# Layer 1's r, v and z projections on one Trainium2 core: TensorE in emission order, with the systems' work at set places between portions of twelve products

## The chip, the cores and the metric

The kernel runs on 1 core of one Trainium2 chip. The metric is the device time of one execution in microseconds. The engines are TensorE (PE, matrix products), VectorE (DVE), ScalarE (ACT), GpSimd (POOL) and SyncE (SP), which issues the DMAs of this kernel. Each engine works its instructions off in its own order, and waits where an operand or a buffer is not ready.

## The reference

One inference step of a trunk with two layers, 1,104 rows (16 meta tokens, 1,024 prompt rows and 8 x 8 sample rows) of width 1,024. Layer 0 is a gated DeltaNet, layer 1 an RWKV-7 time mixing. Of layer 1, with the shapes D = 1024 and 16 heads of 64:

```python
def rwkv_mixer(xn, S0, shift_prev, mu, w_rkvz, w0, w1, w2, a0, a1, a2, k_k, k_a, r_k, lnx_w, lnx_b, w_o):
    xprev = jnp.concatenate([shift_prev[:, None].astype(jnp.float32), xn[:, :-1]], 1)
    xx = xprev - xn
    xs = xn[None] + xx[None] * mu[:, None, None, :]
    rkvz = jnp.einsum('sbtd,sde->sbte', xs[:4], w_rkvz)
    r, k, v, z = rkvz[0], rkvz[1], rkvz[2], rkvz[3]
    w = -jax.nn.softplus(-(w0 + jnp.tanh(xs[4] @ w1) @ w2)) - 0.5
    a = jax.nn.sigmoid(a0 + (xs[5] @ a1) @ a2)
    kk = l2norm((k * k_k).reshape(B, T, H, N))
    ...
    def step(S, inp):
        S = (S * d_t[:, :, None, :]
             + jnp.einsum('bhvk,bhk->bhv', S, -kk_t)[..., None] * b_t[:, :, None, :]
             + v_t[..., None] * k_t[:, :, None, :])
        return S, jnp.einsum('bhvk,bhk->bhv', S, r_t)
```

The kernel doesn't step through the rows. It cuts them into chunks of 64, and for each chunk and head solves a triangular system of 64 x 64 whose matrix comes from the keys kk, the rates a and the decays. Inverting these matrices needs k, a and w alone, not r, v or z, so it can be done while r, v and z are projected.

## The kernel before

The rows stand in three segments of 384, 384 and 336 columns (`SEGS`). Layer 1 first projects k, the decays and the rates (`keys_decay_rate`), then r, v and z, and then runs the wave over the chunks. The part from k's end to the wave's start is the stage of the change.

*Projections.* For each of m = 0 (r), 2 (v) and 3 (z), `mix` builds the shifted input of that m in pairs of tiles (xa, xc, xh are high parts, xl and others low parts), 8 parts a segment: ACT scales (mixs), DVE adds (L1071, L1068), ACT casts to the high part (L86) and DVE or POOL subtracts for the low part (L90). Then `project(m, k, ...)` makes the 8 output tiles. The weights of a tile come in two halves (wraw; `load_w`, L202), split by ACT into whi and by POOL into wlo, three buffers each. A segment's product is 24 matmuls into one tile d in PSUM (`dense`): 8 slices of the inner dimension, each with whi by high, wlo by high and whi by low. ACT copies d to ev (L1155), and SP stores it (L1156). r and v have three segments, z two; z's third is left to the wave, for which `gate_inputs` prepares the input.

*Systems.* There are 24 items (3 segments by 8 pairs of heads), worked on in five batches of 5, 5, 5, 5 and 4 by `rwkv_inverse`, called after the projection tiles 1, 4, 7, 10 and 13 of the 24. An item loads its cs, a and k (sldcs, slda, sldk, L1255), and prepares its keys: sal (DVE, L1273), skk (POOL, then DVE, L1299). PE then makes the scores: 12 small matmuls fL and one product frss with a head mask. The scores are copied (sgl, ACT; rkc, DVE, L1313) and stored to DRAM by SP (rltd, L1311; rssd, L1314). When a batch's items are stored, `block_scale` loads the norms back (invR, L487; bblk, L492), PE transposes invR into fbpp (called bpp here), and DVE forms rk and bblk (L494, L495). `inverse_blocks` loads the blocks of the systems (L21, L456; invA, L461), scales them (L462), inverts 32 x 32 blocks in 31 pairs of DVE steps (`inverse32`, L444 and L446: a batch's inverse), copies (ACT, L464), stores both (r_t, L468, and r_u, L467), and loads them in the form that the merge needs: T1n (L472) and per item sTT (four loads, L478, after a POOL memset, L476). `inverse_merge` joins the blocks of an item: 12 matmuls mY, a DVE scaling into invY (L510, twice), 12 matmuls mU, ACT into sTT, then SP's store ttd (L1322). The wave reads ttd.

*Buffers.* sTT has three buffers for the five items of a batch, so items 3 and 4 wait until the stores ttd of items 0 and 1 have landed. T1n, L21, invT, sal have one buffer, skk and sgl two. PSUM has four buffers for d, two for the f tiles (L, rss, bpp, lora) and two for mY and mU.

*Order.* In this stage a scheduler decides the order of every engine's instructions, PE's too: products of several tiles and the systems' work stand interleaved in it as it estimated them to be ready. The wave behind already stands in a manual order for PE (`tc.manual_schedule`), in which PE's instructions stand as they are emitted.

Of the kernel before, what the change touches and what calls it, by code (L numbers as in the profile page):

```python
# [16 lines left out]
SEGS = [(0, 384), (384, 384), (768, 336)]  # L17
# [18 lines left out]
class Builder:  # L36
# [461 lines left out]
    def inverse_merge(self, L21, TT, T1n, scale_col, pool, th0, n):  # L498

        nc = self.nc  # L500
        pY = self.ps("m", 2, "Y")
        yv = pY[:, 0:32 * n].rearrange("p (c i) -> p c i", i=32)
        for c in range(n):
            for p in (0, 1):
                a = 64 * p
                self.mm(yv[a + 32:a + 64, c, :], L21[a:a + 32, th0 + c, :], T1n[a:a + 32, th0 + c, :])
        Y = self.t(pool, [128, 192], "invY", 2)[:, 0:32 * n].rearrange("p (c i) -> p c i", i=32)
        for p in (0, 1):
            a = 64 * p + 32
            nc.vector.tensor_tensor(Y[a:a + 32], yv[a:a + 32],  # L510
                                    scale_col[a:a + 32].unsqueeze(2).broadcast_to([32, n, 32]), op=ALU.mult)
        pU = self.ps("m", 2, "U")
        uv = pU[:, 0:32 * n].rearrange("p (c i) -> p c i", i=32)
        for c in range(n):
            for p in (0, 1):
                a = 64 * p
                self.mm(uv[a:a + 32, c, :], Y[a + 32:a + 64, c, :], TT[a + 32:a + 64, c, 32:64])
        for p in (0, 1):
            a = 64 * p
            self.act(TT[a:a + 32, :, 32:64], uv[a:a + 32], AF.Identity, scale=-1.0)  # L520
# [621 lines left out]
            self.mm(p[:, 0:n], wl, h[:, c0:c0 + n], start=False, stop=True)  # L1142
            dst(k, s, p)

    def project(self, m, k, x, dst, apart=False):

        nc, t = self.nc, self.t
        w = self.load_w(self.i["rwkv_w_rkvz"][0, m][:, 128 * k:128 * k + 128])
        ps = (self.dense(w, 128, *x, s, bufs=4) for s in range(2 if m == 3 else 3)) if apart else self.dense3(w, 128, *x)
        for (c0, n), p in zip(SEGS, ps):  # L1150
            f = t(self.ev, [128, 384], "ev", 3)
            if m == 3:
                self.gate(f[:, 0:n], p[:, 0:n])
            else:
                nc.scalar.copy(f[:, 0:n], p[:, 0:n])  # L1155
            nc.sync.dma_start(dst[k][:, c0:c0 + n], f[:, 0:n])  # L1156

    def keys_decay_rate(self, x, hh, hl):

        nc, t, i, col = self.nc, self.t, self.i, self.pcol  # L1160
        with self.tc.tile_pool(name="lora", bufs=1, reuse_waits="tile") as pool:
            z = t(pool, [128, 8, 48], "zpad")
            nc.gpsimd.memset(z, 0.0)
            for d in (self.ad, self.rd, self.vd, self.zd, self.kd):
                nc.sync.dma_start(d[:, :, NT:1152].rearrange("k p n -> p k n"), z)
            sm = t(pool, [128, 384], "sm0")
            sm1 = t(pool, [128, 384], "sm1")
            self.scan_mask(sm, True)
            self.scan_mask(sm1, False)

            wr = t(pool, [128, 2, D], "lw2")
            for q in (0, 64):
                nc.sync.dma_start(wr[q:q + 64, 0], i["rwkv_w2"][0])
                nc.sync.dma_start(wr[q:q + 64, 1], i["rwkv_a2"][0])
            w2 = t(pool, [128, 2, D], "lw2h", dt=F32R), t(pool, [128, 2, D], "lw2l", dt=F32R)
            nc.scalar.copy(w2[0], wr)

            for u, q in ((0, slice(0, 64)), (1, slice(64, 128))):
                nc.vector.tensor_tensor(w2[1][q, u], wr[q, u], w2[0][q, u].bitcast(F32), op=ALU.subtract)
                nc.gpsimd.memset(w2[1][64 - q.start:128 - q.start, u].bitcast(F32), 0.0)  # L1180

            def dst_w(k, s, p):
                c0, n = SEGS[s]
                f = t(self.ev, [128, 384], "ev", 3)
                if s == 2:
                    nc.gpsimd.memset(f[:, n:384], 0.0)
                self.act(f[:, 0:n], p[:, 0:n], AF.Sigmoid, bias=col["rwkv_w0"][:, k:k + 1])
                g = t(pool, [128, 384], "ev2", 2)
                nc.vector.tensor_tensor_scan(g, sm if s == 0 else sm1, f, 0.0, op0=ALU.mult, op1=ALU.add)
                nc.sync.dma_start(self.csd[k][:, c0:c0 + 384], g)  # L1190

            def dst_a(k, s, p):
                c0, n = SEGS[s]
                f = t(self.ev, [128, 384], "ev", 3)
                self.act(f[:, 0:n], p[:, 0:n], AF.Sigmoid, bias=col["rwkv_a0"][:, k:k + 1])
                nc.sync.dma_start(self.ad[k][:, c0:c0 + n], f[:, 0:n])
            for k in range(8):
                self.project(1, k, x, self.kd, k in (0,))
                self.lora_second(0, k, hh, w2, dst_w)
                self.lora_second(1, k, hl, w2, dst_a)  # L1200

# [76 lines left out]

    ahead = None

    def rwkv_inverse(self, b, pool):

        items = range(5 * b, min(5 * b + 5, 24))
        nth = 6 * len(items)
        nc, t = self.nc, self.t
        ltd, ssd = self.dram([nth, 128, 64], f"rltd{b}"), self.dram([nth, 128], f"rssd{b}")
        for q, n in enumerate(items):
            s, p = divmod(n, 8)
            names = ("cs", "a", "k")
            ld = self.ahead or self.rwkv_load(n, pool, "s", names)  # L1290
            kk, Dp, iD = self.rwkv_keys(p, ld, pool, "s")

            self.ahead = self.rwkv_load(n + 1, pool, "s", names) if n < 23 else None
            sq = t(pool, [128, 384], "sgl", 2)
            self.act(sq, kk, AF.Square)
            al = t(pool, [128, 6, 64], "sal", 1)
            self.alpha(al, kk, Dp, s, nc.vector)
            nc.gpsimd.tensor_tensor(kk, kk, ld["a"], op=ALU.mult)
            nc.vector.tensor_tensor(kk, kk, iD, op=ALU.mult)  # L1299
            gp = self.ps("f", 2, "L")  # L1300
            ssp = self.ps("f", 2, "rss")
            for c in range(6):
                for h in (0, 1):
                    a = 64 * h
                    self.mm(gp[a:a + 64, 64 * c:64 * c + 64], kk[a:a + 64, 64 * c:64 * c + 64], al[a:a + 64, c, :])
            self.mm(ssp[0:2, 0:384], self.hmask, sq)
            gl = t(pool, [128, 6, 64], "sgl", 2)
            nc.scalar.copy(gl, gp[:, 0:384].rearrange("p (c i) -> p c i", i=64))
            if s == 0:
                nc.gpsimd.tensor_tensor(gl[:, 0, :], gl[:, 0, :], self.m_strs2, op=ALU.mult)  # L1310
            nc.sync.dma_start(ltd[6 * q:6 * q + 6].rearrange("c q i -> q c i"), gl)  # L1311
            kc = t(pool, [2, 384], "rkc", 1)
            nc.vector.tensor_copy(kc, ssp[0:2, 0:384])  # L1313
            nc.sync.dma_start(ssd[6 * q:6 * q + 6].rearrange("c (h i) -> h c i", h=2), kc.rearrange("h (c i) -> h c i", c=6))  # L1314
        rk2 = self.rk2[:, 30 * b:30 * b + nth]
        blk = self.block_scale(ssd, rk2, pool)
        TT = [t(pool, [128, 6, 64], "sTT", 3) for _ in items]
        T1n, L21 = t(pool, [128, 30, 32], "T1n", 1), t(pool, [128, 30, 32], "L21", 1)
        self.inverse_blocks(f"r{b}", ltd, blk, pool, TT, T1n[:, 0:nth], L21[:, 0:nth], nth)
        for q, n in enumerate(items):  # L1320
            self.inverse_merge(L21, TT[q], T1n, rk2[:, 6 * q:6 * q + 6], pool, 6 * q, 6)
            nc.sync.dma_start(self.ttd[n], TT[q].rearrange("p c k -> p (c k)"))  # L1322


    def rwkv_front(self, p, s):
# [415 lines left out]
    def layer1(self, ctx, right, stay, xa, xb, x):  # L1741

        nc, tc = self.nc, self.tc
# [2 lines left out]
        self.keys_decay_rate(x, self.hh, self.hl)  # L1746
        ip = pool("rinv", ctx)
        self.rwkv_masks(ip, True)
        todo = [(m, k) for m in (0, 2, 3) for k in range(8)]
        slots = {0: (0, 1, 2, 3, 4, 5, 9, 10), 2: (6, 7, 8, 0, 1, 2, 9, 10), 3: range(3, 11)}  # L1750
        for n, (m, k) in enumerate(todo):
            if k == 0:
                x = self.mix(m, xb, slots[m], SEGS[0:2] if m == 3 else SEGS)
            self.project(m, k, x, {0: self.rd, 2: self.vd, 3: self.zd}[m], k in range(8))
            if n in (1, 4, 7, 10, 13):
                self.rwkv_inverse((1, 4, 7, 10, 13).index(n), ip)
            if n == 16:
                zin = self.gate_inputs(xa, xb)
        ctx.close()
        right.close()  # L1760
        self.psum_pool()
# [14 lines left out]
        last.close()  # L1776
        ctx.close()
        self.psum.close()

    def wave(self, zin, stay, last, pool):  # L1780

# [109 lines left out]
```

## Time and profile before

| | us |
|---|---|
| median of 3 runs | 2412.91 |
| lowest and highest run | 2412.68, 2417.64 |
| the profiled execution's own time | 2422.7 |
| its span in the profile | 2421.0 |
| mean granted PE clock of that execution | 0.967 |

Beside the lines that the prediction shows, these are the page's chain of waits (the work that ended last, by engine) and its view of the span in 40 slices, of which the stage is about slices 25 to 31:

```profile
PE 17%; DVE 6%; DMA 3%; issue 2%; ACT 1%; POOL 1%; SPq 0%; DVEq 0%; POOLq 0%; ACTq 0%
...
PE   6989999999999999999989998988998888888896
DVE  6868676776868596863347616588894567667654
PEclk9999999999999999999999999999998999999998
```

How rows of the trace are read. A line of a timeline is: start in us, duration in us, engine (SPq is SP's DMA queue), source line, operation, output<-inputs, shapes and count; in brackets the idle time before it and what ended it. A row of a windows view is: the window, its length, then per engine busy us and the count of instructions, the granted PE clock (1.00 is full), the share of DMA engines in use and GB/s. Matmuls are pipelined, so their durations overlap.

### The profile page before, as it was taken

How to read it: one execution, taken by the hardware profiler on the slowest of the kernel's cores; microseconds unless marked ns; L12 is line 12 of the kernel's file. 1: busy time of each engine (PE TensorE's matmuls, PEld its weight loads, DVE VectorE, ACT ScalarE, POOL GpSimd, SP SyncE). 2: the span in 40 equal slices, each digit the busy share in tenths (PEclk: the TensorE clock that was granted, in tenths of full speed). 3: DMA queues.
4: the chain of work that ended last, by engine and by line, in shares of the span. 5: the costliest groups of instructions: out<-in, count | busy, mean ns of one | idle time of the engine just before them, and what ended most of it. 6: DMA issues, size and time to landing. Idle time of an engine off the chain costs nothing. (4 is left out here: it accounts for less than half of the span.)

```text
span 2421.0 us, 54809 instructions
## 1 busy us (share of the span) xinstructions
PE 2213.4 (91%) x19737; PEld 2003.7 (83%) x19737; DVE 1620.5 (67%) x4201; ACT 1279.8 (53%) x3665; POOL 1049.8 (43%) x1446
## 2 busy tenths in 40 slices
PE   6989999999999999999989998988998888888896
PEld 5888989888898989888989898877787676777775
DVE  6868676776868596863347616588894567667654
ACT  5445555555646565565334647474453555666552
POOL 3435343334434353433314424453354555666643
PEclk9999999999999999999999999999998999999998
DMA  3323333323232333353351344666645435555543
GB/s 110 104 74 101 86 109 86 91 76 99 82 108 61 100 96 89 94 160 114 108 137 61 97 172 153 169 160 172 167 122 173 124 107 149 158 163 156 157 131 117
DMA packets 470924, 290.05 MB, mean 120 GB/s; under 512 B 188506, under 2 KB 456027, under 8 KB 470651
## 3 DMA queue, kind: packets, MB, share of 16 engines
q1 hardware_dynamic: 470650, 286.53, 42.0%
q8 instruction: 156, 2.56, 0.5%
q14 instruction: 118, 0.96, 0.1%
HBM read 200.53 MB, written 85.89 MB: 118 GB/s over the span
## 5 line engine op out<-in xcount | busy, mean ns | idle before, releaser
L90 POOL TENSOR_TENSOR wlo<-wraw,whi 128x512 fp32r<-128x512 f32 (+2 forms) x252 | 331.8, 1319 | 379.9 <-ACT whi L86 361.6
L76 PE MATMUL d<-xc,whi 128*128 128x384 f32 (+2 forms) x910 | 258.3, 341 | 4.5 <-POOL xc L90 2.5
L86 ACT CAST whi<-wraw 128x512 fp32r<-128x512 f32 (+2 forms) x252 | 152.0, 605 | 145.4 <-PE dq L76 50.7
L411 DVE SCALAR_TENSOR_TENSOR cvy<-raw,cw,cvy 128x408 f32<-128x408 f32 (+2 forms) x288 | 179.0, 634 | 16.3 <-ACT cvy L62 14.5
L76 PEld LDWEIGHTS d<-xc,whi 128*128 128x128 f32 (+1 forms) x910 | 167.5, 191 | 10.7 <-issue 3.4
L444 DVE TENSOR_TENSOR invtmp<-invA,invT 72x31 f32<-72x31 f32 (+31 forms) x403 | 165.2, 410 | 14.1 <-DMA invA<-ltd 5.3
L446 DVE TENSOR_TENSOR invT<-invT,invtmp 72x31 f32<-72x31 f32 (+31 forms) x403 | 165.7, 411 | 6.6
L76 PE MATMUL dz<-xc,whi 128*128 128x384 f32 (+1 forms) x480 | 148.9, 341 | 0.0
L76 PE MATMUL dv<-xc,whi 128*128 128x384 f32 (+1 forms) x480 | 146.8, 335 | 0.0
L76 PE MATMUL d<-xc,wlo 128*128 128x384 f32 (+2 forms) x428 | 142.3, 341 | 1.4 <-POOL wlo L90 1.4
L76 PE MATMUL d<-xa,whi 128*128 128x384 f32 (+3 forms) x450 | 139.8, 345 | 3.5 <-DVE xa L90 1.7
L860 POOL TENSOR_SCALAR Sb<-Sb,eglb 128x128 f32<-128x128 f32 x128 | 80.1, 643 | 90.4 <-DMA Sb<-in_state_gdn 46.8
L76 PE MATMUL dv<-xa,whi 128*128 128x384 f32 (+1 forms) x288 | 100.0, 347 | 0.1
L76 PE MATMUL dz<-xa,whi 128*128 128x384 f32 (+1 forms) x288 | 100.1, 348 | 0.0
L76 PEld LDWEIGHTS d<-xa,whi 128*128 128x128 f32 (+1 forms) x450 | 83.1, 190 | 11.5 <-issue 4.5
L76 PEld LDWEIGHTS dz<-xc,whi 128*128 128x128 f32 x480 | 89.4, 192 | 0.8
L76 PEld LDWEIGHTS dv<-xc,whi 128*128 128x128 f32 x480 | 88.6, 188 | 0.5 <-issue 0.4
L80 PE MATMUL rA<-UV,G 128*64 128x64 f32 x1152 | 63.6, 240 | 26.0 <-DVE rS L1470 24.0
L76 PE MATMUL d<-xa,wlo 128*128 128x384 f32 (+3 forms) x252 | 85.5, 339 | 0.0
L62 ACT ACTIVATE o<-rA,gcol 128x128 f32<-128x128 f32 x128 | 46.6, 372 | 73.6 <-DVE S L771 73.3
L76 PE MATMUL d<-xh,wlo 128*128 128x384 f32 (+1 forms) x256 | 84.1, 344 | 1.5 <-POOL wlo L90 1.5
L76 PE MATMUL d<-xh,whi 128*128 128x384 f32 (+1 forms) x256 | 84.2, 344 | 0.7 <-ACT whi L86 0.4
(509 smaller groups left out, 7194.7 us busy)
## 6 DMA issues: line engine op xcount, KB each, us to landing
wraw<-in_gdn_w_in SPq DMA_DIRECT2D x96, 256.0 KB
wraw<-in_rwkv_w_rkvz SPq DMA_DIRECT2D x80, 256.0 KB
Sb<-in_state_gdn SPq DMA_DIRECT2D x64, 256.0 KB
wraw<-in_rwkv_w_o SPq DMA_DIRECT2D x40, 256.0 KB
E<-drow SPq DMA_DIRECT2D x24, 384.0 KB
attn<-drow SPq DMA_DIRECT2D x24, 384.0 KB
wraw<-in_gdn_w_out SPq DMA_DIRECT2D x36, 256.0 KB
out_s_gdn<-Sb SPq DMA_DIRECT2D x32, 256.0 KB
```

The lines of the kernel that those rows point to most:

```text
L62: return self.nc.scalar.activation(out, in_, func, bias=bias, scale=scale, **kw)
L76: self.nc.tensor.matmul(out, lhsT, rhs, start=start, stop=stop)
L80: self.nc.tensor.matmul(out, lhsT, rhs, start=start, stop=True, skip_group_check=True)
L86: nc.scalar.copy(hi, x)
L90: e.tensor_tensor(lo, x, hi.bitcast(F32), op=ALU.subtract)
L411: nc.vector.scalar_tensor_tensor(y[:, 0:wd], raw[:, k:k + wd], cw[k], y[:, 0:wd], op0=ALU.mult, op1=ALU.add)
L444: nc.vector.tensor_tensor(tmp, A[:, j, j + 1:32].unsqueeze(2).broadcast_to([nb, n, m]), Tv[:, j, 0:m].unsqueeze(1).broadcast_to([nb, n, m] ...
L446: nc.vector.tensor_tensor(Tv[:, j + 1:32, 0:m], Tv[:, j + 1:32, 0:m], tmp, op=ALU.subtract)
L860: nc.gpsimd.tensor_scalar(Sb[:, u], Sb[:, u], self.eglb[:, hv, 4 * g + u:4 * g + u + 1], None, op0=ALU.mult)
```

## The change

The loop over r, v and z moves into a method `projections`, which stands under `tc.manual_schedule` for PE: PE's order in the stage is now the order of emission. A segment's 24 matmuls are emitted as two portions of twelve, one for each half of the weights, and after each portion `gap()` is called. There are six gaps in a tile of r or v and four in one of z, 128 in all.

`gap()` takes one step of the systems. `rwkv_inverse` is a generator now: for each item, the loads and the keys are emitted, three gaps are left for them, and then the scores stand. Behind a batch's last scores four gaps are left, then the transpose and the whole inverse are emitted. The merges are put off: merge n of a batch starts (mY) 28 + n gaps after the batch's inverse was emitted, and its second half (mU, the store ttd) stands one gap later, behind a `yield` in `inverse_merge`. The orders of DVE, ACT, POOL and SP stay with the scheduler, which now finds PE's order given. Batches follow one another every 19 gaps: each has five items of three gaps, and four gaps before the transpose. The projection of k's first tile keeps its form with an empty gap.

```diff
     def inverse_merge(self, L21, TT, T1n, scale_col, pool, th0, n):
...
+        yield
         pU = self.ps("m", 2, "U")
...
-    def project(self, m, k, x, dst, apart=False):
+    def project(self, m, k, x, dst, gap=None):
...
-        w = self.load_w(self.i["rwkv_w_rkvz"][0, m][:, 128 * k:128 * k + 128])
-        ps = (self.dense(w, 128, *x, s, bufs=4) for s in range(2 if m == 3 else 3)) if apart else self.dense3(w, 128, *x)
-        for (c0, n), p in zip(SEGS, ps):
+        his, los = w = self.load_w(self.i["rwkv_w_rkvz"][0, m][:, 128 * k:128 * k + 128])
+        ps = zip(SEGS, self.dense3(w, 128, *x)) if gap is None else ((c, self.ps("d", 4)) for c in SEGS[0:2 if m == 3 else 3])
+        for (c0, n), p in ps:
+            if gap is not None:
+                c = 0
+                for q in range(8):
+                    wh, wl = his[q // 4][:, q % 4], los[q // 4][:, q % 4]
+                    a, b = x[0][q][:, c0:c0 + n], x[1][q][:, c0:c0 + n]
+                    for l, r in ((wh, a), (wl, a), (wh, b)):
+                        self.mm(p[:, 0:n], l, r, start=c == 0, stop=c == 23)
+                        c += 1
+                    if q % 4 == 3:
+                        gap()
...
-    def rwkv_inverse(self, b, pool):
+    def rwkv_inverse(self, b, pool, merges):
...
+            for _ in range(3):
+                yield
             gp = self.ps("f", 2, "L")
...
+        for _ in range(4):
+            yield
         rk2 = self.rk2[:, 30 * b:30 * b + nth]
...
-        for q, n in enumerate(items):
-            self.inverse_merge(L21, TT[q], T1n, rk2[:, 6 * q:6 * q + 6], pool, 6 * q, 6)
-            nc.sync.dma_start(self.ttd[n], TT[q].rearrange("p c k -> p (c k)"))
+        def merge(q):
+            m = self.inverse_merge(L21, TT[q], T1n, rk2[:, 6 * q:6 * q + 6], pool, 6 * q, 6)
+            next(m)
+            yield
+            next(m, None)
+            nc.sync.dma_start(self.ttd[items[q]], TT[q].rearrange("p c k -> p (c k)"))
+        merges.extend(merge(q) for q in range(len(items)))
...
-        todo = [(m, k) for m in (0, 2, 3) for k in range(8)]
-        for n, (m, k) in enumerate(todo):
-            if k == 0:
-                x = self.mix(m, xb, slots[m], SEGS[0:2] if m == 3 else SEGS)
-            self.project(m, k, x, {0: self.rd, 2: self.vd, 3: self.zd}[m], k in range(8))
-            if n in (1, 4, 7, 10, 13):
-                self.rwkv_inverse((1, 4, 7, 10, 13).index(n), ip)
-            if n == 16:
-                zin = self.gate_inputs(xa, xb)
+        with tc.manual_schedule(engines={mybir.EngineType.PE}):
+            zin = self.projections(xa, xb, ip)
...
+    def projections(self, xa, xb, ip):
+        slots = {0: (0, 1, 2, 3, 4, 5, 9, 10), 2: (6, 7, 8, 0, 1, 2, 9, 10), 3: range(3, 11)}
+        now, wait, under, merges = [0], [], [], []
+        def systems():
+            for b in range(5):
+                yield from self.rwkv_inverse(b, ip, merges)
+                wait.extend((now[0] + 28 + n, m) for n, m in enumerate(merges))
+                merges.clear()
+        sy = systems()
+        def gap():
+            now[0] += 1
+            for m in under:
+                next(m, None)
+            under.clear()
+            while wait and wait[0][0] <= now[0]:
+                m = wait.pop(0)[1]
+                next(m)
+                under.append(m)
+            next(sy, None)
+        for m in (0, 2, 3):
+            x = self.mix(m, xb, slots[m], SEGS[0:2] if m == 3 else SEGS)
+            for k in range(8):
+                self.project(m, k, x, {0: self.rd, 2: self.vd, 3: self.zd}[m], gap)
+                if (m, k) == (3, 0):
+                    zin = self.gate_inputs(xa, xb)
+        while wait or under:
+            gap()
+        return zin
```

More of the change, by code (lines that the diff above doesn't have):

```diff
@@ L1197, in keys_decay_rate @@
             for k in range(8):
-                self.project(1, k, x, self.kd, k in (0,))
+                self.project(1, k, x, self.kd, (lambda: None) if k == 0 else None)
                 self.lora_second(0, k, hh, w2, dst_w)
@@ L1748, in layer1 @@
         self.rwkv_masks(ip, True)
-        todo = [(m, k) for m in (0, 2, 3) for k in range(8)]
-        slots = {0: (0, 1, 2, 3, 4, 5, 9, 10), 2: (6, 7, 8, 0, 1, 2, 9, 10), 3: range(3, 11)}
-        for n, (m, k) in enumerate(todo):
-            if k == 0:
-                x = self.mix(m, xb, slots[m], SEGS[0:2] if m == 3 else SEGS)
-            self.project(m, k, x, {0: self.rd, 2: self.vd, 3: self.zd}[m], k in range(8))
-            if n in (1, 4, 7, 10, 13):
-                self.rwkv_inverse((1, 4, 7, 10, 13).index(n), ip)
-            if n == 16:
-                zin = self.gate_inputs(xa, xb)
+        with tc.manual_schedule(engines={mybir.EngineType.PE}):
+            zin = self.projections(xa, xb, ip)
         ctx.close()
```

## The prediction

> **What bounds the kernel now.** I read the page first, then windows, waits and timelines of the one stage that the change touches.
>
> ```profile
> span 2421.0 us, 54809 instructions
> PE 2213.4 (91%) x19737; PEld 2003.7 (83%) x19737; DVE 1620.5 (67%) x4201; ACT 1279.8 (53%) x3665; POOL 1049.8 (43%) x1446
> ```
>
> TensorE (PE) is busy for 91% of the span. The stage runs from r's first product of tile 0 to z's last product. The windows view over it, over the stretch from bpp(1) to bpp(2) (the transpose into tile bpp that ends batch 1's and batch 2's collection) and over four slices gives busy time by engine, then the granted PE clock:
>
> ```profile
> core 0: us, PE busy (x) PEld busy (x) DVE busy (x) ACT busy (x) POOL busy (x), PEclk, DMA share, GB/s
> 1464.20:1857.30 393.10, 359.46 (x3331) 316.18 (x3329) 284.86 (x599) 205.83 (x444) 171.51 (x256) 0.95 0.61 159
> 1599.41:1660.31 60.90, 54.31 (x561) 46.40 (x559) 56.05 (x115) 39.46 (x91) 30.14 (x39) 0.93 0.68 167
> 1598.00:1602.00 4.00, 4.00 (x52) 3.11 (x52) 3.33 (x9) 2.68 (x6) 1.03 (x1) 0.50 0.31 50
> 1602.00:1606.00 4.00, 4.00 (x16) 3.58 (x15) 3.17 (x5) 3.75 (x9) 3.33 (x4) 0.65 0.70 144
> 1482.00:1486.00 4.00, 2.71 (x9) 2.00 (x8) 2.92 (x6) 4.00 (x10) 2.96 (x6) 0.50 0.45 129
> ```
>
> The stage is 393.1 us: PE is idle for 393.1 − 359.5 = 33.6, and a mean clock of 0.95 costs 0.05 × 393.1 = 19.7 more. PE's own work is then 393.1 − 33.6 − 19.7 = 339.8 us. VectorE (DVE) is close behind where a mix and an inverse meet: 56.05 of 60.9 us. The lines view of PE over the stage (count | busy us, mean ns of one | idle before, and what ended it), its main rows:
>
> ```profile
> L76 PE MATMUL d<-xc,whi 128*128 128x384 f32 (+1 forms) x400 | 115.5, 345 | 2.7 <-POOL xc L90 2.5 <-DVE xc L90 0.2
> L76 PE MATMUL d<-xa,whi 128*128 128x384 f32 (+1 forms) x288 | 83.9, 345 | 3.5 <-DVE xa L90 1.7 <-ACT xa L86 1.3 <-ACT whi L86 0.5
> L76 PE MATMUL d<-xc,wlo 128*128 128x384 f32 (+1 forms) x200 | 69.5, 348 | 1.4 <-POOL wlo L90 1.4
> ...
> L76 PE MATMUL fL<-sal,skk 64*64 64x64 f32 x576 | 25.1, 235 | 11.1 <-DVE skk L1299 11.0
> L76 PE MATMUL frss<-sgl,hmask 128*2 128x384 f32 x48 | 21.3, 527 | 1.9 <-DVE rk L494 1.9
> L76 PE MATMUL mU<-sTT,invY 32*32 32x32 f32 x576 | 16.6, 195 | 3.3 <-ACT mixs L62 1.5 <-DVE invY L510 0.9 <-issue 0.6
> L76 PE MATMUL mY<-T1n,L 32*32 32x32 f32 x576 | 15.3, 196 | 7.4 <-DMA T1n<-r_t 4.7 <-issue 2.7
> ```
>
> Most of the idle time (11.1 + 1.9 + 3.3 + 7.4 = 23.7) is systems' work, scores (fL, frss) and merges (mU, mY), standing ahead of projection products that could have run. That is what the change can win; it cannot win more than 33.6 + 19.7 = 53 us.
>
> **The change part by part.** It adds and removes no instruction. PE's 339.8 us I keep; the regrouping could save some switches between groups, none of which the views show as more than 0.2 us, so I take 0 (bounds 0 and −2). What changes is who waits, since PE now obeys the emission order and does not pass a late operand.
>
> Start. The stage's first waits come from r's mix (POOL xc 2.5, DVE xa 1.7, ACT xa 1.3, flora behind ACT ev 0.5: 6.0 us) and stay. Segment 2 of r needs the mix's last part:
>
> ```profile
> PE flora L76 <- ACT ev L62: 0.5, 1, 0.5
> 1493.25 0.94 POOL L90 TENSOR_TENSOR xl<-mixs,xh 128x336 fp32r<-128x336 f32 x1 [1.28 <-ACT xh L86]
> 1464.20:1494.20 30.00, 22.00 (x95) 0.83 0.49 157
> 1507.30 0.51 PE L76 MATMUL d<-xc,whi 128*128 128x384 f32 x2
> 1507.64 0.34 PE L76 MATMUL d<-xc,wlo 128*128 128x384 f32 x1
> 1544.80 0.47 PE L76 MATMUL d<-xa,whi 128*128 128x336 f32 x2
> 1545.11 0.32 PE L76 MATMUL d<-xa,wlo 128*128 128x336 f32 x1
> ```
>
> It is there at 1494.2. By then PE had done 95 products (third row, tile d alone), as tile r1 filled the hole. In order it can do r0's 72 and item 0's scores. A product of 384 columns takes 0.34/2 = 0.17 us (1507.30 to 1507.64), one of 336 takes 0.31/2 = 0.155. The 23 missing ones are 23 × 0.17 = 3.9; item 0's scores, some 1.5 us, are done earlier instead, which leaves 2.4. (An item is at most (25.1 + 21.3)/24 = 1.9 and a merge (16.6 + 15.3)/24 = 1.3 by busy time, in which the ends of pipelined matmuls overlap; I take 1.5 and 0.9.) I take 3.3 between 1 and 6, since the last of the 24 products cannot all be done by 1494.2. Idle: 9.3.
>
> bpp(1). In the changed order item 9's scores stand, then four portions (some 8 us), then bpp(1). On the DVE the last six steps of inverse 0 stand behind item 9's keys, and on SP the order is r_t store, r_u store, T1n's 2 loads, sTT's 12 loads, item 9's rssd store, invR's load. So bpp(1) now waits for the inverse before it. Its chain, priced by the timelines of ACT, SP and PE:
>
> ```profile
> 1586.85 2.11 ACT L464 COPY invA<-invT 120x1024 f32<-120x1024 f32 x1
> 1586.46 0.35 SPq L468 DMA_DIRECT2D r_t<-invT  x1
> 1588.98 0.35 SPq L467 DMA_DIRECT2D r_u<-invA  x1
> 1589.87 4.29 SPq L472 DMA_DIRECT2D T1n<-r_t  x2
> 1596.20 5.66 SPq L478 DMA_DIRECT2D sTT<-r_u  x12
> 1538.71 0.36 SPq L1314 DMA_DIRECT2D rssd<-rkc  x1
> 1540.77 0.39 SPq L487 DMA_DIRECT2D invR<-rssd  x1
> 1545.67 0.24 PE L73 MATMUL fbpp<-ident,invR 30*128 30x30 f32 x1
> 1819.08 0.33 SPq L467 DMA_DIRECT2D r_u<-invA  x1
> 1822.67 5.79 SPq L478 DMA_DIRECT2D sTT<-r_u  x12
> ```
>
> Six steps of some 0.45 (the inverse's row below has 0.49) with item 10's step between are 2.5 to 3, r_t to r_u 2.5 (the ACT copy of 2.1 between), r_u to the first sTT load 7.2 (3.6 in the last batch), 12 loads 5.7, rssd to invR 2.1, invR to the transpose 4.9: 24.9 us (with 2.5) after item 9's scores, 21.3 with the shorter landing. PE is there after 8 + 1.5 = 9.5. The wait is 15.4 or 11.8; invR's own 4.9 holds a wait for PE's turn, and its store may land sooner, so the bounds are 9 and 16, and I take 12. Behind it on PE stand all further products; behind invR on SP bblk's and invA's loads, so inverse 1 starts as late.
>
> Batch 2. From bpp(1) to bpp(2) PE has 19 portions (38 us at 12 × 0.155 to 0.17), five items at 1.5, five merges at 0.9 and some 2 of switches: 52 us. The DVE order of the changed kernel puts there 62 inverse steps, 44 steps of v's mix, 15 of items and 10 merge scalings; before's 60.9 us held 52, 34, 15 and 10 in 56.05 us of busy time. A step of a mix by itself in the timeline, then the lines view of that stretch:
>
> ```profile
> 1492.88 0.54 DVE L1071 SCALAR_TENSOR_TENSOR mixs<-xb,pcol,mixs 128x320 f32<-128x320 f32 x1
> L1071 DVE SCALAR_TENSOR_TENSOR mixs<-xb,pcol,mixs 128x336 f32<-128x336 f32 (+2 forms) x19 | 14.6, 771 | 0.1
> L446 DVE TENSOR_TENSOR invT<-invT,invtmp 120x156 f32<-120x156 f32 (+15 forms) x26 | 12.7, 487 | 0.4
> ```
>
> Ten steps more of the inverse (at 0.47) and ten of the mix (at some 0.66; its other forms are shorter than the 0.77 above) are 11 us, some 10 of busy time: 66 us against PE's 52, a wait of 14, spread over items 11 to 14 and bpp(2). The same mix step takes 0.54 where nothing stretches it, and at such durations DVE needs some 55: bounds 3 and 19; I take 10.
>
> The rest. Batch 3's rssd stands behind sTT loads that wait for inverse 2, as in batch 1, but the inverse ends sooner there: 3 (0 to 8). The last T1n meets its merge about when PE does: 3 (0 to 6). Items 3 and 4 of each batch reuse sTT buffers whose ttd stores must land: 2 (0 to 8). The T1n wait of batch 0 (4.06 us) and most of the skk waits go, as merges now come 28 portions late.
>
> Clock. The wait for T1n is followed by 8 us at 0.50 and 0.65, thus 2.0 + 1.4 = 3.4 us:
>
> ```profile
> 1597.54 0.24 PE L76 MATMUL mY<-T1n,L 32*32 32x32 f32 x2 [4.06 <-DMA T1n<-r_t]
> 1481.07 0.44 PE L76 MATMUL d<-xc,whi 128*128 128x384 f32 x1 [2.49 <-POOL xc L90]
> 1846.04 0.57 PE L76 MATMUL mU<-sTT,invY 32*32 32x32 f32 x24
> 1860.53 1.42 PE L76 MATMUL fG<-AR,BK 64*128 64x128 f32 x12 [3.19 <-POOL BK L1356]
> ```
>
> One long wait costs such a slump once: 3.4 for bpp(1). The other 27.3 us of idle (9.3 + 10 + 8) I charge as before's, 19.7/33.6 = 0.586 each: 16.0.
>
> In the Trainium skill, "TensorE: Matmul & The Clock Gate", Part 1, the clock halves only after an idle window of about 3.4 us. The trace differs: 0.50 stands in 1482 to 1486 after a wait of 2.49. By the page's rule alone only bpp(1) would pay.
>
> End. After the last merge's mU before has 60 products (1846.0 to 1857.3); the changed order has 36. SP's first load for the wave stands behind that merge's ttd store in both, so the wave's first fG comes 24 × 0.17 = 4.1 us later against z's end (bounds 0, if later waits of the wave take it up, and 4.1).
>
> Sum: 339.8 + (9.3 + 12 + 10 + 8 = 39.3) + (3.4 + 16.0) = 398.5 against 393.1, thus +5.4; with the end +9.5. The profiled execution took 2422.7 (span 2421.0), so it would take 2432.2. The runs' median, 2412.9, lies 9.8 below the profiled one; I carry the difference over: 2422.4, forecast as 2422.
>
> **The rivals.**
> *Faster: the queues keep up.* If DVE runs the mix at its bare durations, batch 2 waits 3, the 8 of the rest vanish, and bpp(1) costs 8: idle 20.3, clock 3.4 + 12.3 × 0.586 = 10.6, stage 339.8 + 30.9 = 370.7; −22.4 + 4.1 = −18, thus 2395. For it: 9% of DVE stays idle even in its densest stretch. Against it: the SP order of bpp(1), which DVE's speed does not mend.
> *Slower still: the mix is the bound.* Batch 2 at its upper 19: 9 × 1.586 = 14.3 more, 2437. It decides as soon as DVE's work from bpp(1) to bpp(2) passes PE's 52 us, and each 0.1 us on its 106 inverse and mix steps is 11 us. Against it: the DVE order is only a queue, and with PE waiting some of POOL's load falls away.
> *It does not do what it says.* The waits change names, not their sum: gains at T1n, skk and the late merges pay for bpp(1): 2413. For it: both orders hold the same work and the same chain of inverses.
> *Short waits cost no clock.* If only a wait as long as bpp(1)'s lowered the clock, by half of 3.4 us, the clock term would be 1.7 in place of 19.4: 2422.4 − 17.7 = 2404.7. Against it: the 0.50 after 2.49 us.
>
> **How the numbers follow.** The measurement tells 0.2%, some 4.8 us. My forecast, 2410 to 2434 in its own range, has 0.45 (slower 0.38, within 0.2% 0.07). The faster rival has 0.26 (faster 0.25, same 0.01), the slower one 0.14, no net change 0.12 (same 0.08, slower 0.02, faster 0.02), the short waits 0.03. Together faster 0.30, same 0.16, slower 0.54. The range reaches from the faster rival, 2395, to the slower one with a little beyond, 2441.
>
> **What would show it.** Right: PE idle of 9 us or more before bpp(1), released by invR's load, with sTT's loads ahead of it on SP; waits of fL on skk between bpp(1) and bpp(2) with DVE over 90% busy; no T1n wait in batch 0; the wave's first fG some 7.4 us behind z's last product; r0's segment 2 waiting for xl. Wrong: bpp(1) not waiting, a stage shorter than 390 us, or a clock near 1.00 through it. A large wait on weights (whi, wlo) would be one that I priced at nothing: in before these are 0.5 and 1.4 us.

## The result, and the profile after

The changed kernel takes 2436.97 us (median of 4 runs, 2436.13 to 2443.59) beside 2412.8 us for the kernel before: a ratio of 1.0114, 95% interval 1.0085 to 1.0143 (the quotient of the two medians is 1.0100; the ratio on record is not formed from them). A second series, e12 below, gave 1.0093 (1.0069 to 1.0117). It is slower by about 1%. The profiled execution took 2437.49 us, its span is 2435.8.

The windows view of the changed kernel, over the stage (r's first product to z's last) and from bpp(1) to bpp(2); columns as before:

```profile
core 0: us, PE busy (x) PEld busy (x) DVE busy (x) ACT busy (x) POOL busy (x), PEclk, DMA share, GB/s
1463.45:1874.10 410.65, 361.89 (x3319) 320.96 (x3319) 283.14 (x590) 203.28 (x437) 171.46 (x251) 0.92 0.58 150
...
1585.60:1661.42 75.82, 62.88 (x599) 53.01 (x600) 64.59 (x131) 46.33 (x107) 39.74 (x43) 0.86 0.56 136
```

The stage grew from 393.1 to 410.65 us, thus by 17.6. PE is idle for 410.65 − 361.89 = 48.8 us in place of 33.6: 15.2 of the 17.6. The mean clock fell from 0.95 to 0.92. By busy time that is 0.08 × 361.9 = 29.0 us against 0.05 × 359.5 = 18.0, which would leave PE's own work 8.6 us shorter; a mean of two digits can't carry that difference (see e8), so clock and own work together are the remaining 2.4. The waits view of PE, from the stage to the wave's start:

```profile
engine line waited for: us in total, times, longest us
PE fbpp L73 <- DMA invR<-rssd: 18.2, 4, 6.7
PE fG L76 <- POOL BK L1378: 7.3, 1, 7.3
PE fL L76 <- DVE skk L1312: 6.3, 3, 2.8
PE mU L76 <- DVE invY L510: 5.0, 3, 4.0
...
PE mU L76 <- ACT siD L62: 3.0, 2, 2.3
...
PE mU L76 <- ACT mixs L62: 2.0, 1, 2.0
PE mU L76 <- issue: 1.4, 1, 1.4
...
PE mU L76 <- ACT sTT L62: 1.1, 1, 1.1
```

Waits for T1n (mY) and for rk (frss) are gone, and the skk waits fell from 11.0 to 6.3. In their place stand the transposes, 18.2 us against 1.2, and the second halves of the merges, 5.0 + 3.0 + 2.0 + 1.4 + 1.1 = 12.5 against 3.3. The four late transposes in PE's timeline, with four slices of the windows view:

```profile
1585.60 0.28 PE L73 MATMUL fbpp<-ident,invR 30*128 30x30 f32 x1 [5.80 <-DMA invR<-rssd]
1661.42 0.28 PE L73 MATMUL fbpp<-ident,invR 30*128 30x30 f32 x1 [3.67 <-DMA invR<-rssd]
1727.01 0.28 PE L73 MATMUL fbpp<-ident,invR 30*128 30x30 f32 x1 [6.71 <-DMA invR<-rssd]
1779.40 0.21 PE L73 MATMUL fbpp<-ident,invR 24*128 24x24 f32 x1 [1.97 <-DMA invR<-rssd]
```

```profile
1778.00:1782.00 4.00, 2.60 (x9) 2.59 (x10) 3.21 (x8) 3.60 (x9) 2.58 (x6) 0.69 0.30 61
...
1722.00:1726.00 4.00, 0.00 (x0) 0.00 (x0) 0.00 (x0) 0.00 (x0) 0.34 (x1) 0.86 0.44 117
1726.00:1730.00 4.00, 3.00 (x11) 2.96 (x12) 1.06 (x4) 0.00 (x0) 0.00 (x0) 0.50 0.85 123
1730.00:1734.00 4.00, 4.00 (x21) 4.00 (x20) 0.38 (x1) 0.96 (x2) 1.29 (x1) 0.78 0.92 196
```

From 1722 to 1726 no engine but POOL does anything: PE waits for a load, and DVE and ACT stand idle too. After it PE runs at 0.50; around the shorter wait before 1779.40 the mean is 0.69. What the load waits for is in the queue of SP. Ahead of bpp(1), item 9's scores on PE, the copy of its norms on DVE, and SP's timeline:

```profile
1569.05 0.91 PE L76 MATMUL fL<-sal,skk 64*64 64x64 f32 x24
1570.74 0.55 DVE L1328 COPY rkc<-frss 2x384 f32<-2x384 f32 x1
...
1569.87 0.35 SPq L468 DMA_DIRECT2D r_t<-invT  x1
1571.96 0.35 SPq L467 DMA_DIRECT2D r_u<-invA  x1
...
1576.03 0.49 SPq L1267 DMA_DIRECT2D sldk<-kd  x1
1576.62 5.78 SPq L478 DMA_DIRECT2D sTT<-r_u  x12
1582.50 0.25 SPq L1329 DMA_DIRECT2D rssd<-rkc  x1
1582.85 0.81 SPq L1168 DMA_DIRECT2D rd<-ev  x2
1583.79 0.39 SPq L487 DMA_DIRECT2D invR<-rssd  x1
```

The store of item 9's norms (rssd) stands behind twelve sTT loads, which stand behind the stores of inverse 0 (r_t, r_u). The norms were ready at 1571.3 and left at 1582.5; 5.8 of these 11.2 us are the issue of the twelve loads. It is the same before bpp(3), with the twelve loads from 1718.08 and rssd at 1723.99. These two are 12.5 of the 18.2 us. Before bpp(2) and bpp(4) the twelve loads don't stand in the way; there invR's load follows the norms' last store by 3.2 and 9.0 us, with other DMAs of SP between. At the end PE's and SP's timelines show z's last product beginning at 1873.75 and:

```profile
1866.99 0.57 PE L76 MATMUL mU<-sTT,invY 32*32 32x32 f32 x24
1881.38 1.01 PE L76 MATMUL fG<-AR,BK 64*128 64x128 f32 x6 [7.29 <-POOL BK L1378]
```

```profile
1868.34 0.32 SPq L1343 DMA_DIRECT2D ttd<-sTT  x1
1868.70 0.42 SPq L1267 DMA_DIRECT2D fldcs<-csd  x1
```

The wave begins at 1881.38, 20.9 us later than before (1860.53).

### The profile page after: what moved, and what is told of

Read it like the earlier page. It is cut to its first block, busy times and chain, and to the rows that moved or that the text cites. A ratio compares the mean times of both kernels' runs of the same rounds, so it can differ in the third digit from the quotient of the medians.

```text
span 2435.8 us, 54790 instructions
## 1 busy us (share of the span) xinstructions
PE 2214.3 (91%) x19737; PEld 2008.3 (82%) x19737; DVE 1622.1 (67%) x4201; ACT 1281.5 (53%) x3665; POOL 1051.2 (43%) x1446
## 5 line engine op out<-in xcount | busy, mean ns | idle before, releaser
L76 PE MATMUL d<-xc,whi 128*128 128x384 f32 (+2 forms) x910 | 264.8, 346 | 2.7 <-ACT ev L1167 1.8
L411 DVE SCALAR_TENSOR_TENSOR cvy<-raw,cw,cvy 128x408 f32<-128x408 f32 (+2 forms) x288 | 180.2, 639 | 17.0 <-ACT cvy L62 15.2
L76 PE MATMUL d<-xa,whi 128*128 128x384 f32 (+3 forms) x450 | 145.7, 354 | 3.4 <-ACT xa L86 2.0
L76 PEld LDWEIGHTS d<-xc,wlo 128*128 128x128 f32 (+1 forms) x428 | 82.4, 194 | 3.6 <-POOL wlo L90 3.2
```

Of the source, the lines that this page charges most:

```text
L76: self.nc.tensor.matmul(out, lhsT, rhs, start=start, stop=stop)
L411: nc.vector.scalar_tensor_tensor(y[:, 0:wd], raw[:, k:k + wd], cw[k], y[:, 0:wd], op0=ALU.mult, op1=ALU.add)
```

## The experiments

All of them are edits of the changed kernel, but for e8. Ratios are to the kernel before, with 95% intervals.

**e1: the changed emission, PE's order left to the scheduler.**

```diff
-        with tc.manual_schedule(engines={mybir.EngineType.PE}):
-            zin = self.projections(xa, xb, ip)
+        zin = self.projections(xa, xb, ip)
```

> The changed kernel's emission (portions, gaps, late merges) without the manual order for PE: the scheduler places PE's instructions again. Theory (PE's fixed order is what costs): PE passes late operands again, no wait before a transpose above 1.5 us, stage near before's 393 us, median 2408 to 2420. Rival A (the emission itself costs, as merges 28 portions late and generators shift the DVE's and SP's order): the waits change place but the stage stays above 403 us, median above 2427.

Measured: 1.0019 (1.0000 to 1.0039). Windows view of the stage and PE's waits for invR and before the wave:

```profile
1464.00:1855.10 391.10, 357.11 (x3345) 313.39 (x3343) 286.49 (x588) 206.41 (x442) 166.08 (x233) 0.97 0.60 157
```

```profile
PE fbpp L73 <- DMA invR<-rssd: 1.7, 2, 1.3
```

```profile
1868.82 1.65 PE L76 MATMUL fG<-AR,BK 64*128 64x128 f32 x12 [13.85 <-POOL BK L1378]
```

With the same portions, gaps and late merges, the stage is back at before's length once PE may pass a late operand. So the fixed order on PE costs, and rival A falls. The last merge stands at the very end here, and the wave waits 13.85 us. Its first fG is 8.2 us later than e8's, but its span ends 0.2 us after e8's (2417.8 and 2417.6): in this pair of traces the wave took that lag back.

**e2: the norms' stores and loads issued by ACT.**

```diff
-            nc.sync.dma_start(ssd[6 * q:6 * q + 6].rearrange("c (h i) -> h c i", h=2), kc.rearrange("h (c i) -> h c i", c=6))
+            nc.scalar.dma_start(ssd[6 * q:6 * q + 6].rearrange("c (h i) -> h c i", h=2), kc.rearrange("h (c i) -> h c i", c=6))
...
-        nc.sync.dma_start(row, ssd)
+        nc.scalar.dma_start(row, ssd)
...
-            nc.sync.dma_start(blk[2 * n * r:2 * n * r + 2 * n], ssd.rearrange("c (p r i) -> r (c p) i", p=2, r=2)[r])
+            nc.scalar.dma_start(blk[2 * n * r:2 * n * r + 2 * n], ssd.rearrange("c (p r i) -> r (c p) i", p=2, r=2)[r])
```

> The changed kernel with the norms' stores (rssd) and the loads of invR and bblk issued by ACT in place of SP, so they no longer stand behind the sTT loads that wait for the inverse. Theory (SP's order makes the transposes late): of the 18.2 us of waits for invR at least 12 go, and some 8 of low clock with them, median 2414 to 2422. Rival A (DVE is late anyway): the waits before the transposes go, but as much comes back before fL or mU, median above 2431. Rival B: ACT waits at these stores itself and holds up the copies of d, slower than 2437.

Measured: 1.0024 (1.0006 to 1.0042), median 2422.68, just above the theory's 2414 to 2422. The timeline of all engines ahead of bpp(1), and the windows of the stage and from bpp(1) to bpp(2):

```profile
1576.72 0.24 ACTq L1329 DMA_DIRECT2D rssd<-rkc  x1
1580.88 5.90 SPq L478 DMA_DIRECT2D sTT<-r_u  x12
1582.94 0.35 ACTq L487 DMA_DIRECT2D invR<-rssd  x1
...
1584.78 0.21 PE L73 MATMUL fbpp<-ident,invR 30*128 30x30 f32 x1 [0.80 <-ACT ev L1167]
```

```profile
1463.45:1860.70 397.25, 360.18 (x3331) 316.20 (x3329) 286.58 (x592) 206.38 (x442) 169.74 (x253) 0.94 0.59 156
```

```profile
1584.78:1657.81 73.03, 60.80 (x600) 50.57 (x600) 63.17 (x126) 46.30 (x107) 34.68 (x43) 0.91 0.62 154
```

The norms now go out 4 us ahead of the sTT loads, and the wait before bpp(1) is 0.80 us, ended by ACT and not by the load. Of 18.2 us for invR 1.7 are left, and the stage is 13.4 us shorter. Three kinds of DMA moved off SP give back most of the loss while PE's order stays fixed: with PE's order fixed, the queue was the cause, as rivals A and B would not have it. The loss thus takes both, the fixed order (e1) and the queue. From bpp(1) to bpp(2) the stretch is still 73.0 us, with 12.2 of PE idle.

**e3: the transpose and the inverse three portions later, merges at their old places.**

```diff
-        rk2 = self.rk2[:, 30 * b:30 * b + nth]
-        blk = self.block_scale(ssd, rk2, pool)
...
+        def tail():
+            rk2 = self.rk2[:, 30 * b:30 * b + nth]
+            blk = self.block_scale(ssd, rk2, pool)
...
+            if q == 0 and self.tail:
+                self.tail()
             gp = self.ps("f", 2, "L")
...
-                wait.extend((now[0] + 28 + n, m) for n, m in enumerate(merges))
+                yield from self.rwkv_inverse(b, ip, lambda ms: wait.extend((now[0] + 25 + n, m) for n, m in enumerate(ms)))
```

> The changed kernel with each transpose and inverse emitted three portions later, just ahead of the next batch's first scores, the merges at their old places. Theory (the transposes come too soon for their operand): waits of 5.8, 3.7, 6.7 and 2.0 shrink by up to three portions, 6.2 us, each, thus nearly all of the 18.2 us and the clock after them, median 2414 to 2424. Rival: the operand comes later too, as the loads move with the emission, or the merges now lack the three portions: waits for T1n or invY of over 8 us in all, median 2432 or more.

Measured: 1.0055 (1.0022 to 1.0088), median 2429.73, between the theory's range (up to 2424) and the rival's (from 2432). The wait for invR fell to 3.3 us in one place, but the scores behind it now wait for rk (4.8 us), for skk (3.1) and for ACT (3.1), and one product 3.5 us for weights. The stage is 399.3 us. About half of the loss went: part of each wait was really covered by three portions, part was handed on to the next instruction in the fixed order.

**e4: two portions between the halves of a merge.**

```diff
-            for m in under:
-                next(m, None)
-            under.clear()
+            while under and under[0][0] <= now[0]:
+                next(under.pop(0)[1], None)
...
-                under.append(m)
+                under.append((now[0] + 2, m))
...
-                wait.extend((now[0] + 28 + n, m) for n, m in enumerate(merges))
+                wait.extend((now[0] + 27 + n, m) for n, m in enumerate(merges))
```

> The changed kernel with two portions, not one, between the halves of a merge: mY one portion sooner, mU at its place. Theory (one portion of 2 us is too little for the DVE's two scalings in its queue): of the 12.5 us of waits before mU (invY 5.0, ACT 6.1, issue 1.4) half goes, 6 us and some 4 of clock, median 2425 to 2431. Rival (mU waits for ACT and DVE queues that are late as a whole): the same waits stand elsewhere, median 2434 to 2440.

Measured: 1.0128 (1.0102 to 1.0153), median 2448.7, above the ranges of both the theory and the rival: no gain. PE's waits view:

```profile
PE mY L76 <- DVE invY L510: 5.8, 5, 2.0
...
PE mU L76 <- ACT sTT L62: 1.9, 1, 1.9
PE mU L76 <- issue: 1.4, 1, 1.4
```

The mU waits fell from 12.5 to some 3.6 us, and mY waits in their place. By the code, mY and mU share two PSUM buffers, so the third mY needs the buffer that the scaling of the second gives free, and that scaling is as young as it was for mU. More buffers were not tried. The waits for weights (wlo) rose too, from 2.0 to 5.4 us.

**e5: e1 with the last batch's merges six portions sooner; e6: e2 with four; e10: e1 with four; e11: e10 with the norms on ACT.** The edit, with 22 in e5 and 24 in the others:

```diff
-                wait.extend((now[0] + 28 + n, m) for n, m in enumerate(merges))
+                wait.extend((now[0] + (22 if b == 4 else 28) + n, m) for n, m in enumerate(merges))
```

> The free order of e1 with the last batch's four merges six portions sooner, so that PE still has z products when the last ttd store lands. In e1 the wave's first fG stands 13.9 us idle, in before 3.2. Theory (SP's loads for the wave stand behind the last ttd store): the wait falls by 6 to 12 us to 2 to 8, and the time by as much as its clock and the wave pass on, ratio to before 0.994 to 1.000. Rival (the wave takes it back later, or T1n is not there that early and PE waits): ratio above 1.000.

> e2 (manual order, the norms' stores and loads on ACT) with the last merges four portions sooner. Theory: the wait before fG falls from 6.7 to about 2, ratio to before from 1.0024 to 1.000 (0.997 to 1.002). Rival: T1n of the last batch comes later than the merge then stands, a new wait for T1n of 2 to 8 us on PE, ratio 1.003 or more.

> e5 with the last merges four portions sooner than the changed kernel's, not six. e5 had a new wait for T1n of 2.4 us and still 3.2 at fG. Theory: the T1n wait goes, the wait at fG grows to at most 7; ratio to before 0.996 to 1.000, as e5 within noise. Rival: the wave is held up by the full four us, ratio 1.001.

> e10 with the norms' stores and loads on ACT: does freeing SP gain anything where PE may pass a late transpose? Theory (it gains only where PE waits in order): no gain, ratio to before 0.996 to 1.001, equal to e10 within 0.3%. Rival (inverses start sooner, so merges and keys are less late): 0.4% or more below e10.

Measured: e5 0.9984 (0.9966 to 1.0001), e6 1.0018 (0.9999 to 1.0037), e10 1.0022 (1.0005 to 1.0038), e11 1.0021 (1.0002 to 1.0040). The wait before fG is 3.18 us in e5, 7.34 in e10, 0.89 in e6. In e6 the gain is lost two groups of products on:

```profile
1871.41 0.66 PE L76 MATMUL fbonus<-prh,bones 128*128 128x384 f32 x1 [5.29 <-DVE G L1408]
```

So the wait does follow the last merge's place, and little of it reaches the end. e10 fell to its rival: expected was a ratio of 0.996 to 1.000, as e5, and with the merges four portions sooner instead of six its interval lies above e5's. e5 is the best version tried; its interval touches 1, so it is not shown to beat the kernel before. e11 equals e10: freeing SP gains nothing where PE may pass the transpose.

**e7: without the mix for v, which is projected from r's mixed input instead.**

```diff
-            x = self.mix(m, xb, slots[m], SEGS[0:2] if m == 3 else SEGS)
+            if m != 2:
+                x = self.mix(m, xb, slots[m], SEGS[0:2] if m == 3 else SEGS)
```

> The changed kernel without the mix for v: v is projected from r's mixed input, which leaves out 24 parts of the mix (some 44 DVE steps of 0.54 to 0.77 us, and ACT's) beside inverse 1. Theory of the prediction (DVE is the bound between bpp(1) and bpp(2)): that stretch falls from 75.8 us to PE's own 55 or less, ratio to before from 1.0114 to about 1.003, and the waits of bpp(1) and bpp(3) stay. Rival (SP's queue makes the stretch long): bpp(2) still waits 3 us or more, the stretch stays above 65.

Measured: 1.0099 (1.0076 to 1.0122); the stretch from bpp(1) to bpp(2) is 66.2 us. SP's and PE's timelines at bpp(2):

```profile
1642.57 6.67 SPq L478 DMA_DIRECT2D sTT<-r_u  x12
1649.83 0.35 SPq L1329 DMA_DIRECT2D rssd<-rkc  x1
1651.70 0.37 SPq L487 DMA_DIRECT2D invR<-rssd  x1
```

```profile
1654.62 0.28 PE L73 MATMUL fbpp<-ident,invR 30*128 30x30 f32 x1 [8.31 <-DMA invR<-rssd]
```

The mix gone, inverse 1 ends sooner, and the scheduler puts its sTT loads ahead of the norms in this batch too. One wait stepped into the place of another. The marks of the rival came (a stretch above 65 us, a wait of 8.3 us at bpp(2)), but with that wait in the mix's place the run could not tell whether the mix was a bound.

**e9: e2 and e7 together.**

> e2 (the norms' stores and loads on ACT) without the mix for v, which leaves out 24 parts of the mix: v is projected from r's mixed input. In e7 SP's queue put a wait of 8.3 us at bpp(2) in the mix's place, so it could not tell. Theory (with SP out of the way DVE and ACT with the mix are what stretches bpp(1) to bpp(2)): the stretch falls from e2's 73.0 us to 54 to 60, and what is left of its waits, 12 us, to under 4; ratio to before 0.994 to 0.999. Rival (merges and keys are late for their own sake): the stretch stays above 66, ratio 1.001 or more.

Measured: the stretch falls to 59.4 us, the ratio is 1.0036 (1.0015 to 1.0057). The window from bpp(1) to bpp(2):

```profile
1577.63:1637.01 59.38, 55.22 (x600) 48.14 (x600) 40.20 (x92) 24.60 (x52) 19.04 (x33) 0.97 0.73 188
```

PE's idle time there fell from e2's 12.2 to 4.2 us, DVE's work from 63.2 to 40.2. So the mix beside the inverse does stretch batch 2, as the prediction had it, once SP's queue is out of the way; ACT's share of the mix went with it, so the run does not part DVE from ACT. The wave's first fG comes at 1856.50, 4 us ahead of before's, yet the runs are not faster, against the expected 0.994 to 0.999. The profiled execution ends 1.4 us ahead of e8's (2416.2 and 2417.6), so part of the lead is lost in the wave; the rest of the difference, and where it arises, was not followed.

**e8: the kernel before once more; e12: the changed kernel once more.** No edit.

> The kernel before, once more, for a second profile. The first took 2422.7 us while its other runs took 2407 to 2418; from the wave's first fG to the end it has 560.5 us, the changed kernel 554.4. If the first profile is drawn out in the wave, this one shows 552 to 556 there and the same stage of 393 +- 2; if the wave is shorter because of the change, it shows 560 again.

> The changed kernel once more. Its profile lies 18.2 us behind the second profile of the kernel before at the wave's last tiles (ratio 1.0075), while its first four runs gave 1.0114 (1.0085 to 1.0143) against four runs of before, whose median is some 3 us lower than in later sessions. If the profiles tell the size, the ratio is 1.007 to 1.009; if an effect outside the stage is missing, it stays at 1.011 or above. The stage's waits (18 us for invR in four places) come again in the same places either way.

Measured: e8 0.9998 (0.9982 to 1.0014), e12 1.0093 (1.0069 to 1.0117). The stage of e8, and the first row of e12's waits:

```profile
1464.20:1857.40 393.20, 360.07 (x3377) 319.12 (x3375) 287.51 (x603) 210.80 (x454) 173.22 (x258) 0.97 0.61 162
```

```profile
PE fbpp L73 <- DMA invR<-rssd: 19.5, 4, 7.6
```

Both kernels repeat their stage, and the waits for invR are a property of the changed kernel. From fG to the end e8 has 557.0 us, between the two outcomes expected, 3.5 less than in before's first profile (560.5). Against e8 the changed kernel lies 19.8 us behind at the wave's first transpose of v and 18.2 at the end (2435.8 against 2417.6). The two series' intervals are 20.5 to 34.5 and 16.6 to 28.2 us (the ratios by 2412.8); this pair of traces lies within the second alone. e12's own trace ends at 2440.1, 22.5 us behind e8's and within both; it is 4.2 us behind the changed kernel's first trace before the stage begins (r's first product at 1467.66 and 1463.45) and 4.3 at the end, so the loss in the stage is the same. Beside before's first trace (2421.0) the two lie 14.8 and 19.1 us behind. So the loss is some 15 to 28 us, and closer than that it isn't settled. e12's ratio is close to the first of the two outcomes expected (1.007 to 1.009; the other began at 1.011).

## Why the prediction was right in direction and short in size

Forecast were +9.5 us and slower; measured are 15 to 23 us in the pairs of traces and, by the ratios, 22 (e12) and 28 (the first runs). The whole range held the time. The forecast's own range, 2410 to 2434, did not, and 2437 is the time given to the rival "the mix is the bound". That agreement is in the main luck: the rival had 19 us of idle time in batch 2, where 12.9 were measured, and the excess lies in bpp(3), bpp(4) and the merges, as told below. Its condition did hold, DVE's work in that stretch being 64.6 us against the 52 priced for PE. By the prediction's steps:

- *Start*, idle 9.3. The waits view to 1496 sums to 9.7, 0.8 of it at the very edge. The sum is right by luck: the mix's first waits came to 4.8 us, not 6.0, those of r0's segment 2 (for xc, xh and xl) to 2.2, not 3.3, and 2.8 us for item 0's skk, which I had not priced, fill the gap.
- *bpp(1)*, 12, between 9 and 16. The mechanism was right, e2 shows it; the size was 5.8, below the lower bound and below the 9 us that I gave as a sign. The chain's terms, from the start of item 9's scores (1569.05), with what I had priced in brackets: r_t stored after 0.8 us (2.5), r_u after 2.1 more (2.5), the first sTT load after 4.7 (7.2 or 3.6), rssd behind the twelve loads after 5.9 (5.7), invR after 1.3 (2.1), the transpose after 1.8 (4.9). Together 16.6 in place of 24.9 or 21.3, while PE was there after 10.8 in place of 9.5. The inverse had thus all but ended when item 9's scores began, and the two largest misses are before's prices for invR's landing and for the way from r_u to sTT.
- *Batch 2*, 10, between 3 and 19. Idle in the stretch is 75.82 − 62.88 = 12.9, of which 3.7 at bpp(2), 4.4 before mU and 2.3 before fL for skk. Right in size, and e9 shows that the mix is behind most of it; but the sign that I gave, waits for skk with DVE over 90% busy, came only as that one wait, with DVE busy for 64.59 of 75.82 us, 85%.
- *The rest*, 8. Here the idle term was too small. bpp(3) waited 6.7, not 3, and bpp(4), priced at nothing, 2.0. T1n, priced at 3, did not wait. The merges were the miss: I had let them wait only for sTT's buffers (2 us), since they come 28 portions late. But their halves stand one portion of 2 us apart, and mU waits for DVE's and ACT's queues, 12.5 us in all, of which some 4 lie in batch 2. e4 shows that a second portion alone does not mend it.
- Together idle 48.8 in place of 39.3: this is 9.5 of the 12.2 by which the stage (+17.6 against +5.4) was underrated.
- *Clock and own work*, 19.4 and 339.8 in the sum. Together they are 410.65 − 48.8 = 361.9 in place of 359.2, thus 2.7 more. The clock alone by its mean is 29.0. No such term is safe: I had priced idle time by before's mean clock of 0.95, at 0.586 us of clock for each us of idle. e8 has the same stage at 0.97, and by the same working that is 0.03 × 393.2 = 11.8 us of clock for 33.1 of idle, 0.36 each, and 348 us of own work in place of 339.8.
- *End*, +4.1. The wait before fG grew from 3.19 to 7.29: right to the tenth, and by the mechanism named, the wave's first load (fldcs, 1868.70) standing behind the last ttd store (1868.34). How much of such a lag reaches the end the runs don't settle: e1's trace ends level with e8's in spite of it, and e6's gain there is lost again.

The rival "the queues keep up" fell: batch 2 was idle for 12.9 us, not 3, and the waits of the rest grew. "It does not do what it says" fell by the two intervals, which both lie above 1. "Short waits cost no clock" fell as well: around the wait of 1.97 us at 1779 the granted clock is 0.69 in 1778 to 1782, by finer slices 1.00 in 1776 to 1778 and 0.50 in 1780.5 to 1782. The Trainium skill's idle window of about 3.4 us ("TensorE: Matmul & The Clock Gate", Part 1) is thus no safe bound here. Not every wait of that size does this: after one of 2.32 us, before fL at 1613.61, it is 1.00 up to 1618.

## What to carry to other kernels

A fixed order on the busiest engine can turn a late operand into idle time of that engine, so each place must be priced with the whole chain behind it, the DMA queue included: a small store on SP stood behind twelve loads of another batch, and moving it and the loads that depend on it to another issuer made the stage 13 us shorter. Where two halves of a job share few buffers, spacing them out in time moves the wait to the next half. Before an engine is named as the bound, take away the queue in front of it too: e7 and e9 differ in that alone.

## What was not expected of the hardware

The mean granted clock of a stage is no measure of time by itself: the kernel before has 0.95 in one profile and 0.97 in the other, with stages of 393.1 and 393.2 us. And the wave's length is no constant: from its first fG to the end the traces have 557.0 and 560.5 us in the kernel before, 554.4 in the changed one, 549.0 in e1, which starts it 8 us late, and 555.2 in e2, which starts it 7 us late. What in it sets this was not tried.
